# A two-layer streaming encoder: half-wide products in three PSUM banks, a second transpose bank, loads in place

## The chip, the cores and the metric

The kernel runs on one core of one Trainium2 chip. The metric is the device time of one execution in microseconds (us): the span from the program's first to its last instruction and what lies around it. Several executions are timed and their median is taken. A profile is one further execution with its own time.

## The reference

One inference step of a trunk of two layers, model width 2048, all in float32. 512 prompt frames and 64 sample frames go through together, 576 tokens. Layer 1 has stick-breaking attention (16 heads of 64) beside a Mamba-2 block (32 heads of 64, state 128); layer 2 has chunk-band attention (32 heads of 64, own chunk of 64 and 8 chunks back, a relative bias per head). Each layer has one input projection, SiLU gates, one output projection and a LayerNorm. Cut to what matters here:

```python
def odd_layer(x, past_k, past_v, w_in, rel_bias, w_out, ln_g, ln_b):
    q, k, v, g = jnp.split(jnp.einsum('bld,de->ble', x, w_in), 4, axis=-1)
    o = chunk_band_attention(q, k, v, past_k, past_v, rel_bias) * jax.nn.silu(g)
    y = layer_norm(DEEPNORM_ALPHA * x + jnp.einsum('ble,ed->bld', o, w_out), ln_g, ln_b)
# per head and block of 64 queries, inside chunk_band_attention:
    s = jnp.where(mc, einsum('bqhd,bkhd->bhqk', qc, kc) * CA_HEAD_DIM ** -0.5 + bias, -inf)
    out = einsum('bhqk,bkhd->bqhd', softmax(s), vc)
```

The outputs are the new activations, the new key and value rows, and the new states.

## The kernel before, in words

**Layout.** Activations stand transposed: 16 tiles of 128 features by 576 tokens. A **product** (`product`, `terms`, L107 to L124) makes 128 output features: two weight tiles of 128x1024 are loaded to `raw` (two buffers, 512 KB each, on SP's queue), and `split` (L88 to L94) makes a high part on ScalarE (`wh`, L93) and the rest on VectorE (`wl`, L94), three buffers each. For each of 16 blocks of 128 features three matmuls (high x high, high x low, low x high) run on each half of the tokens, 288 columns each: 96 matmuls. The two halves lie in two neighbouring banks of one `pj` tile. There are two `pj` tiles, four of the eight PSUM banks.

**Order.** The program is written in one order of pairs and steps, and a scheduler lays out each engine's list when the kernel is built, by a timing of its own. It fills waits of one step with instructions of others, such as matmuls of later products. On the chip every engine and queue follows its list strictly.

**Stages, in order of time in the span.**
- 0 to 655 us: layer 1's Mamba block. 655 to 1180: layer 1's attention, 8 pairs of heads.
- 1150 to 1500: `mix_norm` (L736 on): `bring` loads 24 stored tiles, 8 of them through two staging tiles `raws` and 16 through the unused tiles `d[4:]`, into high and low tiles `oh`, `ol` (L758 to L760). The output projection then runs. Its last `NHALF0 = 6` output tiles are made half by half of the tokens (L834): first half of all six, its statistics, then the second half, while VectorE and ScalarE normalise the first half. Weights of these tiles are loaded and split once for each half.
- 1490 to 1545: `two_of_seven` (L162): 2 block products for each of the first five query/key pairs, on the first token half alone, with results kept in `vs` tiles and stored. Then `early_values`: three value products.
- 1580 to 1925: `seven` (L176): query and key projections of layer 2 by a scheme with 7 block products (M1 to M7) of 24 matmuls for 16 pairs; the first five pairs have M1 and M2 already. A block product waits for a sum of weight tiles on VectorE and their split. For early pairs M7 and M4 go into the same bank `pa`, with the add at L223 reading it in between.
- 1925 to 2520: layer 2's attention, 16 pairs (`run_pairs`, L608). For each pair: `ca_heads` loads operands and makes the value product (evicted as `vf` at L534). Then the gate product, except for pairs in `GLATE`, whose gate comes after all pairs. `silu` reads the gate's `pj` tile three times (L130, L133, L135) and writes `gt`, of which there is one buffer. `ca_attend`: scores `z` (L490, two banks), softmax (L1057 to L1065), transposes of the weights (`transpose_tile`, `transpose_cached`, `transpose_new`, L571 to L589) into one bank with the tag `t`, from which VectorE (L567) and ScalarE (L569) evict by turns, then the product with the values (`po`, L596). `place` multiplies with `gt` (L636, L643).
- 2520 to the end: layer 2's `mix_norm`, with `NHALF1 = 3`, and the final norm: subtractions on GpSimd (L890), multiplications on VectorE (L891), scale and shift on ScalarE (L895), stores (L897).

**Queues.** Loads are issued by SP, all stores by GpSimd's queue (`store`, L58).

**PSUM in layer 2's attention:** four banks in two `pj` tiles, two for scores, one for `po` and the turned values, one for transposes.

Of the kernel before, what the change touches and what calls it, by code (L numbers as in the profile page):

```python
# [14 lines left out]
P = 128  # L15
# [13 lines left out]
GLATE = (10, 12, 14, 15)  # L29
NHALF0, NHALF1 = 6, 3  # L30
# [19 lines left out]
def encoder(ctx: ExitStack, tc: tile.TileContext, a):  # L50
# [7 lines left out]
    store = nc.gpsimd.dma_start  # L58
# [103 lines left out]
    def two_of_seven(w, m0, x1, x2, pl, dst):  # L162
# [5 lines left out]
        m1, c11 = (pl.tile([P, HALF], F32, tag="vs", name="vs", bufs=3) for _ in range(2))  # L168
# [7 lines left out]
    def seven(wa, m0, wb, m1, sums, ps, tmp, last=False, early=None):  # L176
# [21 lines left out]
        c11, c12, c21, c22 = o0[:, H0], o0[:, H1], o1[:, H0], o1[:, H1]  # L198
        if early is None:
            a12 = raw(wa, m0, 1, "raw", wpool, 2)  # L200
# [6 lines left out]
            pb = bank("pb")  # L207
            block(pb, a12, sums["M2"])
            tt(c11, c11, pb, ALU.add)
        else:  # L210
# [3 lines left out]
            a12 = raw(wa, m0, 1, "raw", wpool, 2)  # L214
# [9 lines left out]
        if last:  # L224
            tt(c21, c21, pa, ALU.add)
        tt(s_, a12, s_, ALU.subtract)
        block(pc, s_, sums["M3"], False, True)
        tt(c12, c12, pc, ALU.add)
        if not last:
            block(pa, a22, sums["M4"], False, True)  # L230
            out(c21, pa)
# [332 lines left out]
    def evict(dst, src):  # L564
        flip[0] ^= 1
        if flip[0]:
            nc.vector.tensor_copy(dst, src)  # L567
        else:
            act(dst, src, AF.Copy)  # L569

    def transpose_tile(wsrc, r, t, wts, flipq=False):  # L571

        nb = t + 1
        tp = pm.tile([P, 512], F32, tag="t", name="tpw")
# [5 lines left out]
    def transpose_new(wsrc, dst):  # L580
        tp = pm.tile([P, 512], F32, tag="t", name="tpn")
        nc.tensor.transpose(tp[0:TS, 0:P], wsrc, ident)
        evict(dst, tp[0:TS, 0:P])

    def transpose_cached(wsrc, dst):
        tp = pm.tile([P, 512], F32, tag="t", name="tpw")
# [21 lines left out]
    def run_pairs(lt, npair, late, heads, attend, wg, gate0, scr):  # L608
        pend = []
        for pr in range(npair):  # L610
            st = heads(pr)
            if pr not in late:
                pg = product(wg, gate0 + pr, 2, xh, xl)
                gt = lt.tile([P, T], F32, tag="gt", name="gt", bufs=1)
                silu(lt, pg, gt, T, "st")
# [7 lines left out]
        for pr, o in pend:  # L623
            pg = product(wg, gate0 + pr, 2, xh, xl)
            gt = lt.tile([P, T], F32, tag="gt", name="gt", bufs=1)
            silu(lt, pg, gt, T, "st")
            tt(o, o, gt, ALU.mult)
# [100 lines left out]
    run_pairs(bl_, NPAIR_SB, range(4, 8), sb_heads, sb_attend, a["w_in0"], 24, o_scr0[16:24])  # L728
# [7 lines left out]
    def mix_norm(nk, scr, w, res, gcol, bcol, cut, nhalf, out, beside=None):  # L736
# [9 lines left out]
        ddp = pool("dd", bufs=1, side="left")  # L746
        dd = ddp.tile([P, NK, T], F32, name="d")
        d = [dd[:, m, :] for m in range(NK)]
# [4 lines left out]
        def bring(pl, ks, stage):  # L753
# [8 lines left out]
        bring(oa, range(3), raws)  # L762
        ob = pool("ob", bufs=1, side="left")
        bring(ob, range(3, 8), raws)
        dp = pool("d", bufs=1, side="left")
        s1, s2, cm, mu = (dp.tile([P, T], F32, name=n) for n in ("s1", "s2", "cm", "mu"))
        bring(orr, range(8, nk), d[4:])
# [93 lines left out]
        def norm(ms, v):  # L861

            r = dd[:, ms.start:ms.stop, v]
# [8 lines left out]
        if inner:  # L872
            yp = pool("x1", bufs=1, side="right")
            yh, yl = (yp.tile([P, NK, T], F32R, name=n) for n in ("yh", "yl"))
            steps = beside(yh, yl, dp)
# [9 lines left out]
        else:  # L885
            for h, v in enumerate(toks):
                for m in range(NK):
# [8 lines left out]
                    if m % 2:  # L896
                        store(out[m - 1:m + 1, :, v].rearrange("m p t -> p m t"), dd[:, m - 1:m + 1, v])  # L897
# [5 lines left out]
        ob.release()  # L903
        oa.release()
        if inner:
            return yp, yh, yl, ddp, dd
        ddp.release()

    def early_pairs(hi, lo, pl):
        x = [[(hi[:, 8 * u + k, H0], lo[:, 8 * u + k, H0]) for k in range(8)] for u in range(2)]  # L910
        for pr in range(NAHEAD):
            yield from two_of_seven(a["w_in1"], pr, *x, pl, e_scr[pr])

    xp, yh, yl, ddp, ys = mix_norm(24, o_scr0, a["w_out0"], a["xT"], V_G0, V_B0, HALF, NHALF0, y_scr,
# [5 lines left out]
    vp = pool("vs", bufs=1, side="left")  # L920
# [286 lines left out]
```

## Time and profile before

| what | value |
|---|---|
| median of 3 runs (lowest, highest) | 2764.26 us (2759.38, 2769.35) |
| the profiled execution | 2769.17 us |
| its span | 2767.2 us |
| mean granted TensorE clock | 0.983 of full speed |
| TensorE busy (PE) | 2663.6 us, 96% |
| VectorE (DVE), ScalarE (ACT), GpSimd (POOL) busy | 59%, 43%, 8% |

Busy time of an engine is the time in which at least one of its instructions ran. Matmuls overlap each other in the trace, so their durations are longer than the distance from one to the next. "Idle before" a group of instructions names what ended the wait. The clock's two levels are 2.4 and 1.2 GHz; a clock of 0.94 for a stretch is a mean over parts at one level and at the other.

### The profile page before, as it was taken

How to read it: one execution, taken by the hardware profiler on the slowest of the kernel's cores; microseconds unless marked ns; L12 is line 12 of the kernel's file. 1: busy time of each engine (PE TensorE's matmuls, PEld its weight loads, DVE VectorE, ACT ScalarE, POOL GpSimd, SP SyncE). 2: the span in 40 equal slices, each digit the busy share in tenths (PEclk: the TensorE clock that was granted, in tenths of full speed). 3: DMA queues.
4: the chain of work that ended last, by engine and by line, in shares of the span. 5: the costliest groups of instructions: out<-in, count | busy, mean ns of one | idle time of the engine just before them, and what ended most of it. 6: DMA issues, size and time to landing. Idle time of an engine off the chain costs nothing.

```text
span 2767.2 us, 47827 instructions
## 1 busy us (share of the span) xinstructions
PE 2663.6 (96%) x19742; PEld 2536.1 (92%) x19742; DVE 1626.2 (59%) x2504; ACT 1197.1 (43%) x1976; POOL 209.3 (8%) x402
## 2 busy tenths in 40 slices
PE   8999999999999999999998899999999999998995
PEld 8999898999999999999998899999998899887995
DVE  6665656665556766643356677666555544564546
ACT  5434343434555665622244434444444433453224
POOL 0000010000000000000000111111000000000005
PEclk9999999999999999999999899999999999999998
DMA  5222232223323222443355565444745555544333
GB/s 186 77 88 80 65 102 65 94 70 118 97 90 97 97 90 90 155 128 101 101 175 171 171 200 175 159 158 161 227 141 155 162 151 162 154 129 154 107 108 120
DMA packets 126953, 355.07 MB, mean 128 GB/s; under 512 B 22400, under 2 KB 29184, under 8 KB 126736
## 3 DMA queue, kind: packets, MB, share of 16 engines
q1 hardware_dynamic: 107424, 286.40, 33.6%
q0 software_dynamic: 19312, 65.63, 6.1%
q8 instruction: 155, 2.54, 0.4%
q14 instruction: 62, 0.51, 0.1%
HBM read 286.34 MB, written 65.61 MB: 127 GB/s over the span
## 4 chain that ended last, share of the span: by engine, by line
PE 87%; DVE 5%; DMA 4%; ACT 2%; issue 1%; SPq 0%; POOLq 0%; POOL 0%; DVEq 0%; ACTq 0%
PE pj L124 59%; PE pa L159 5%; PE po L596 3%; PE pc L159 3%; PE pj L834 2%; PE tpw L576 2%; DMA sr<-w_in 1%; DVE wl L94 1%; PE z L490 1%; PE px L834 1%; PE pb L159 1%; PE z L491 1%; PE px L124 1%; PE pe L159 1%; ACT wh L93 1%
## 5 line engine op out<-in xcount | busy, mean ns | idle before, releaser
L93 ACT ACTIVATE wh<-raw 128x1024 fp32r<-128x1024 f32 x381 | 402.7, 1058 | 743.9 <-PE pj L124 521.7
L94 DVE TENSOR_TENSOR wl<-raw,wh 128x1024 fp32r<-128x1024 f32 x381 | 467.3, 1227 | 426.3 <-ACT wh L93 421.1
L124 PE MATMUL pj<-yh,wh 128*128 128x288 f32 x1024 | 227.0, 300 | 4.9 <-DVE vf L534 3.6
L124 PE MATMUL pj<-yh,wl 128*128 128x288 f32 x1024 | 225.0, 297 | 0.0
L124 PE MATMUL pj<-yl,wh 128*128 128x288 f32 x1024 | 223.3, 298 | 0.0
L124 PE MATMUL pj<-oh,wh 128*128 128x288 f32 x816 | 175.1, 297 | 5.9 <-ACT oh L759 4.0
L124 PE MATMUL pj<-ol,wh 128*128 128x288 f32 x816 | 175.4, 296 | 0.3 <-DVE ol L760 0.3
L124 PEld LDWEIGHTS pj<-yh,wh 128*128 128x128 f32 x1024 | 165.9, 188 | 9.6 <-DVE vf L534 5.0
L124 PE MATMUL pj<-oh,wl 128*128 128x288 f32 x816 | 174.5, 296 | 0.0
L124 PEld LDWEIGHTS pj<-yl,wh 128*128 128x128 f32 x1024 | 166.2, 188 | 2.1
L124 PEld LDWEIGHTS pj<-yh,wl 128*128 128x128 f32 x1024 | 166.9, 188 | 0.9
L124 PEld LDWEIGHTS pj<-oh,wh 128*128 128x128 f32 x816 | 131.4, 189 | 7.3 <-ACT oh L759 4.7
L124 PEld LDWEIGHTS pj<-ol,wh 128*128 128x128 f32 x816 | 131.5, 189 | 0.6 <-DVE ol L760 0.5
L124 PEld LDWEIGHTS pj<-oh,wl 128*128 128x128 f32 x816 | 131.9, 189 | 0.0
L567 DVE COPY wts<-tpw 128x128 f32<-128x128 f32 (+1 forms) x96 | 46.9, 488 | 113.0 <-PE tpw L576 112.8
L1061 ACT ACTIVATE t<-t,smx 128x128 f32<-128x128 f32 (+3 forms) x128 | 71.3, 558 | 50.9 <-DVE smx L1057 50.6
L596 PE MATMUL po<-wts,vt 128*64 128x512 f32 (+3 forms) x384 | 86.6, 460 | 0.0
L1057 DVE CUSTOM_DVE_ANT_0 t<-z,bp 128x128 f32<-128x128 f32 (+3 forms) x128 | 60.8, 486 | 43.0 <-PE tpw L576 33.0
L834 PE MATMUL pj<-oh,wh 128*128 128x288 f32 (+2 forms) x256 | 77.4, 302 | 5.1 <-DVE d L783 2.6
L834 PE MATMUL pj<-oh,wl 128*128 128x288 f32 (+2 forms) x256 | 77.4, 302 | 2.0 <-DVE wl L94 2.0
L834 PE MATMUL pj<-ol,wh 128*128 128x288 f32 (+2 forms) x256 | 76.2, 298 | 0.0
L490 PE MATMUL z<-kh,q 128*128 128x128 f32 (+1 forms) x192 | 66.5, 360 | 6.6 <-DVE smx L1057 5.1
(572 smaller groups left out, 7380.7 us busy)
## 6 DMA issues: line engine op xcount, KB each, us to landing
raw<-w_in SPq DMA_DIRECT2D x234, 512.0 KB, 3.6
raw<-w_out SPq DMA_DIRECT2D x104, 512.0 KB, 3.6
sr<-w_in SPq DMA_DIRECT2D x48, 512.0 KB, 4.3
q<-q_scr SPq DMA_DIRECT2D x64, 128.0 KB, 3.5
kh<-k_scr SPq DMA_DIRECT2D x64, 128.0 KB, 3.4
xr<-xT SPq DMA_DIRECT2D x26, 288.0 KB, 6.0
o_scr<-of POOLq DMA_DIRECT2D x24, 288.0 KB, 3.6
d<-o_scr SPq DMA_DIRECT2D x24, 288.0 KB, 5.6
```

The source lines that it names most:

```text
L93: act(hi, src, AF.Copy)
L94: tt(lo, src, hi.bitcast(F32), ALU.subtract)
L124: mm(ps[:, at.start + v.start:at.start + v.stop], st[:, c], mv[u * 8 + k][:, v], start=(first and k == 0 and i == 0), stop=(last and k == ...
L159: mm(acc, st[:, c], mv, start=(first and k == 0 and i == 0), stop=(k == 7 and i == 2), skip_group_check=more)
L490: mm(dst, q, kh, start=True, stop=False)
L491: mm(dst, q, kl, start=False, stop=True)
L567: nc.vector.tensor_copy(dst, src)
L576: nc.tensor.transpose(tp[:, b * P:(b + 1) * P], wsrc[:, b * P:(b + 1) * P], ident)
L596: mm(po[q, b * P:TP], vt[:, b, q], wts[:, b, r, b * P:TP], start=(b == 0), stop=(b == 3))
L834: mm(ps[i], st[:, c], mv, start=(u == order[0] and k == 0 and j == 0), stop=(u == 0 and k == 7 and j == 2))
L1057: nc.vector.tensor_tensor_reduce(t[:, i, at:at + z.shape[1]], z, b, -1.0, 3e38 if j == 0 else sm[:, i:i + 1], ALU.add, ALU.min, sm[:, i:i ...
L1061: act(t[:, i, :], t[:, i, :], AF.Exp, scale=-1.0, bias=sm[:, i:i + 1], accum_out=sm[:, 2 + i:3 + i])
```

## The change

1. Stores are issued by ScalarE's queue.
2. `seven` is reordered: for early pairs M3 comes ahead of M7, and M4 has a bank of its own, `pb`; for the others M2 follows M6. The tile `a12` is loaded first.
3. In `mix_norm` each stored tile is loaded straight into its `ol` tile and converted there; `d` is four tiles of four instead of one; `NHALF0` is 3. The tiles kept by `two_of_seven` and `early_values` come from two `stage` tiles, and the memory under them is laid out in another order (`oa` below `d`).
4. Layer 2's value and gate products run one token half after the other, in three banks by turns. The fourth bank of the two tiles is a second transpose bank, used by turns. Late gates are those of pairs 9, 11, 13, 15.

```diff
-GLATE = (10, 12, 14, 15)
-NHALF0, NHALF1 = 6, 3
+GLATE = (9, 11, 13, 15)
+NHALF0, NHALF1 = 3, 3
...
-    store = nc.gpsimd.dma_start
+    store = nc.scalar.dma_start
...
+        a12 = raw(wa, m0, 1, "raw", wpool, 2)
         if early is None:
...
-            pb = bank("pb")
-            block(pb, a12, sums["M2"])
-            tt(c11, c11, pb, ALU.add)
...
         block(pa, s_, sums["M6"], early is not None, early is None)
         out(c12, pa)
+        tt(s_, a12, s_, ALU.subtract)
+        pb = bank("pb")
+        if early is None:
+            block(pb, a12, sums["M2"])
+            tt(c11, c11, pb, ALU.add)
+        else:
+            block(pc, s_, sums["M3"], False, True)
+            tt(c12, c12, pc, ALU.add)
         tt(a21, a11, a21, ALU.subtract)
         block(pa, a21, sums["M7"], False, True)
         tt(c22, c22, pa, ALU.add)
...
+        else:
+            tt(c21, u1, pa, ALU.add)
+            block(pb, a22, sums["M4"])
+            tt(c21, c21, pb, ALU.add)
...
+    def tbank(name):
+
+        if spare:
+            flip[0] ^= 2
+            if flip[0] & 2:
+                return spare[0]
+        return pm.tile([P, 512], F32, tag="t", name=name)
...
-        raws = [oa.tile([P, T], F32, name=f"or{k}") for k in range(2)]
...
-                raw = stage[k % len(stage)]
+                raw = lo[k].bitcast(F32)
                 load(raw, scr[k])
                 act(hi[k], raw, AF.Copy)
                 tt(lo[k], raw, hi[k].bitcast(F32), ALU.subtract)
...
+        stage = [oa.tile([P, T], F32, name=f"stage{i}") for i in range(2)] if inner else None
+        bring(oa, range(1))
+        ddp = pool("dd", bufs=1, side="left")
+        dg = [ddp.tile([P, 4, T], F32, name=f"d{g}") for g in range(4)]
...
+    x0, x1 = (pj.tile([P, 1024], F32, tag="pj", name="pj") for _ in range(2))
+    hbanks, second = [x0[:, 0:HALF], x0[:, 512:512 + HALF], x1[:, 0:HALF]], x1[:, 512:1024]
+    turn_ = [0]
+
+    def product_halves(w, m):
+
+        ws = [wparts(w, m, u) for u in range(2)]
+        accs = []
+        for v in (H0, H1):
+            acc = hbanks[turn_[0] % 3]
+            turn_[0] += 1
+            for u, (wh, wl) in enumerate(ws):
+                for k in range(8):
+                    c = slice(k * P, (k + 1) * P)
+                    x, y = xh[8 * u + k][:, v], xl[8 * u + k][:, v]
+                    for i, (st, mv) in enumerate(((wh, x), (wh, y), (wl, x))):
+                        mm(acc, st[:, c], mv, start=(u == 0 and k == 0 and i == 0), stop=(u == 1 and k == 7 and i == 2))
+            accs.append((v, acc))
+        return accs
+
+    def silu_halves(pl, accs, dst, tag):
+        t = pl.tile([P, 580], F32, tag=tag, name=tag, bufs=2)[:, :T]
+        for v, p in accs:
+            act(t[:, v], p, AF.Abs)
+        act(t, t, AF.Exp, scale=-1.0)
+        act(t, t, AF.Ln, bias=one1)
+        for v, p in accs:
+            stt(t[:, v], p, 0.0, t[:, v], ALU.min, ALU.subtract)
+        act(t, t, AF.Exp)
+        for v, p in accs:
+            tt(dst[:, v], p, t[:, v], ALU.mult)
+
     pm = pool("pmc", bufs=1, space=PSUM)
+    spare.append(second)
```

## Rows read from the trace of the kernel before

**Rows 1.** The page: the span, and busy time of each engine.

```profile
span 2767.2 us, 47827 instructions
PE 2663.6 (96%) x19742; PEld 2536.1 (92%) x19742; DVE 1626.2 (59%) x2504; ACT 1197.1 (43%) x1976; POOL 209.3 (8%) x402
```

**Rows 2.** Stretches: length, PE, PEld, DVE, ACT, POOL busy, clock, DMA share, GB/s.

```profile
1366.00:1500.00 134.00, 125.40 (x901) 121.64 (x900) 80.07 (x95) 57.48 (x73) 3.58 (x5) 0.99 0.54 170
1500.00:1580.00 80.00, 73.14 (x512) 71.57 (x511) 53.96 (x47) 38.54 (x49) 10.09 (x17) 0.96 0.48 158
1580.00:1700.00 120.00, 108.73 (x780) 107.11 (x779) 87.83 (x99) 45.45 (x56) 22.07 (x41) 0.94 0.61 202
1700.00:1925.00 225.00, 223.61 (x1678) 222.28 (x1677) 152.64 (x164) 101.13 (x147) 35.47 (x66) 1.00 0.46 153
1925.00:2450.00 525.00, 509.62 (x3750) 464.87 (x3749) 271.39 (x723) 220.90 (x505) 35.57 (x68) 0.99 0.55 167
2450.00:2520.00 70.00, 61.42 (x427) 50.06 (x425) 39.87 (x107) 31.98 (x75) 3.23 (x6) 0.90 0.38 121
```

**Rows 3.** The chain that ended last: one whole product of 96 matmuls (start, us).

```profile
1192.78 12.93 PE pj L124 x96
```

**Rows 4.** TensorE's waits, 1160 to 1190 us: us in total, times, longest.

```profile
PE pj L124 <- ACT oh L759: 3.1, 1, 3.1
```

**Rows 5.** Three short stretches, columns as in rows 2.

```profile
1505.00:1545.00 40.00, 33.14 (x218) 31.99 (x217) 37.35 (x36) 24.57 (x37) 7.95 (x13) 0.91 0.60 195
1582.50:1592.70 10.20, 5.71 (x22) 5.37 (x23) 7.35 (x7) 3.06 (x3) 0.10 (x1) 0.50 0.68 209
2504.10:2517.70 13.60, 9.42 (x29) 5.02 (x31) 3.60 (x10) 2.45 (x6) 0.14 (x1) 0.50 0.53 179
```

**Rows 6.** TensorE's waits, 1366 to 1700 us: us in total, times, longest.

```profile
PE pc L159 <- ACT wh L93: 6.0, 1, 6.0
PE pa L159 <- DVE so L223: 4.8, 5, 2.2
PE pe L159 <- DVE vs L173: 3.3, 1, 3.3
```

**Rows 7.** SP's queue, its waits from 1570 to 1590 us.

```profile
SPq L182 <- DVE yl L951: 19.4, 1, 19.4
```

**Rows 8.** Timeline of VectorE (start, us): the last read of a gate's banks.

```profile
2042.04 0.76 DVE L135 TENSOR_TENSOR gt<-pj,st 128x576 f32<-128x576 f32 x1
```

**Rows 9.** Timeline of TensorE, 2502 to 2515 us: the last pair ([idle before]).

```profile
2509.86 1.11 PE L576 MATMUL tpw<-cst,t 128*128 128x128 f32 x4 [1.07 <-DVE wts L567]
2511.66 0.90 PE L576 MATMUL tpw<-cst,t 128*128 128x128 f32 x3 [0.69 <-ACT wts L569]
```

**Rows 10.** Timeline of TensorE, 2441 to 2452 us: two batches of transposes.

```profile
2444.60 0.38 PE L576 MATMUL tpw<-cst,t 128*128 128x128 f32 x2
...
2448.02 0.38 PE L576 MATMUL tpw<-cst,t 128*128 128x128 f32 x2
```

**Rows 11.** DMA issues: first and last of 23 lines of stores, 262 in all.

```profile
o_scr<-of POOLq DMA_DIRECT2D x24, 288.0 KB, 3.6
...
o_conv<-cvo POOLq DMA_DIRECT2D x1, 72.0 KB, 3.4
```

**Rows 12.** Timeline of SP's queue, 2038 to 2042 us: two issues.

```profile
2039.92 0.59 SPq L1015 DMA_DIRECT2D kl<-k_scr  x1
2041.50 0.33 SPq L1044 DMA_DIRECT2D cv<-cav  x1
```

**Rows 13.** Timeline of GpSimd, 2715 to 2768 us: the final norm.

```profile
2744.06 9.35 POOL L890 TENSOR_TENSOR d<-d,mu 128x256 f32<-128x256 f32 x11 [2.38 <-DVE mu L856]
2753.36 1.45 POOL L897 DMA_DIRECT2D o_y<-d  x2
2754.82 0.76 POOL L890 TENSOR_TENSOR d<-d,mu 128x256 f32<-128x256 f32 x1
```

**Rows 14.** Timeline of ScalarE: a gate's first read of its banks.

```profile
2005.92 0.63 ACT L130 ACTIVATE st<-pj 128x576 f32<-128x576 f32 x1
```

More of the change, by code (lines that the diff above doesn't have):

```diff
@@ L167, in two_of_seven @@
         yield
-        m1, c11 = (pl.tile([P, HALF], F32, tag="vs", name="vs", bufs=3) for _ in range(2))
+        m1, c11 = pl
         act(m1, pa, AF.Copy)
@@ L223, in seven @@
         tt(c22, c22, pa, ALU.add)
[L224 to L231, printed above, removed]
+        if early is None:
+            if last:
+                tt(c21, c21, pa, ALU.add)
+            block(pc, s_, sums["M3"], False, True)
+            tt(c12, c12, pc, ALU.add)
+            if not last:
+                block(pa, a22, sums["M4"], False, True)
+                act(c21, pa, AF.Copy)
+        else:
+            tt(c21, u1, pa, ALU.add)
+            block(pb, a22, sums["M4"])
+            tt(c21, c21, pb, ALU.add)
         return o0, o1
@@ L606, in sample_pv, with run_pairs @@
         return po[:, 0:TS]
-    def run_pairs(lt, npair, late, heads, attend, wg, gate0, scr):
+    def run_pairs(lt, npair, late, heads, attend, gate, scr):
         pend = []
@@ L612, in run_pairs @@
             if pr not in late:
-                pg = product(wg, gate0 + pr, 2, xh, xl)
-                gt = lt.tile([P, T], F32, tag="gt", name="gt", bufs=1)
-                silu(lt, pg, gt, T, "st")
+                gt = gate(lt, pr)
             else:
@@ L623, in run_pairs @@
         for pr, o in pend:
[L624 to L627, printed above, removed]
+            tt(o, o, gate(lt, pr), ALU.mult)
             store(scr[pr], o)
@@ L745, in mix_norm, with bring @@
         orr = pool("or", bufs=1, side="right")
-        ddp = pool("dd", bufs=1, side="left")
-        dd = ddp.tile([P, NK, T], F32, name="d")
-        d = [dd[:, m, :] for m in range(NK)]
         oa = pool("oa", bufs=1, side="left")
-        raws = [oa.tile([P, T], F32, name=f"or{k}") for k in range(2)]
         hi, lo = [None] * nk, [None] * nk
-        def bring(pl, ks, stage):
+        def bring(pl, ks):
             for k in ks:
@@ L861, in norm @@
         def norm(ms, v):
-            r = dd[:, ms.start:ms.stop, v]
+            r = dg[ms.start // 4][:, :, v]
             n = [[0, ms.stop - ms.start], [1, v.stop - v.start]]
@@ L874, in mix_norm @@
             yh, yl = (yp.tile([P, NK, T], F32R, name=n) for n in ("yh", "yl"))
-            steps = beside(yh, yl, dp)
+            steps = beside(yh, yl, stage)
             for h, v in enumerate(toks):
@@ L911, in early_pairs @@
         for pr in range(NAHEAD):
-            yield from two_of_seven(a["w_in1"], pr, *x, pl, e_scr[pr])
-    xp, yh, yl, ddp, ys = mix_norm(24, o_scr0, a["w_out0"], a["xT"], V_G0, V_B0, HALF, NHALF0, y_scr,
+            t = pl[pr % 2]
+            yield from two_of_seven(a["w_in1"], pr, *x, (t[:, H0], t[:, H1]), e_scr[pr])
+    xp, yh, yl, left, ys, stage = mix_norm(24, o_scr0, a["w_out0"], a["xT"], V_G0, V_B0, HALF, NHALF0, y_scr,
                                    early_pairs)
@@ L928, in early_values @@
                     yield
-            vs = vp.tile([P, T], F32, tag="vs", name="vs", bufs=2)
+            vs = stage[i % 2]
             act(vs, ps[:, parts(HALF)[1]], AF.Copy)
```

57 lines of the change are left out of this document (35 added, 22 removed).

## The prediction

> **What bounds the kernel now.** I read the page first: TensorE is busy for 2663.6 of 2767.2 us [rows 1], and the change takes no matmul away. What can be won is TensorE's 103.6 idle us and what it loses at the lower clock. The view by stretches says where: 8.6, 6.9 and 11.3 us idle between 1366 and 1700 us, 15.4 and 8.6 us in layer 2's attention, and 1.4 us in the 225 us between [rows 2]. There the clock falls too: 0.96 over 80 us costs 3.2 us of work, 0.94 over 120 us 7.2, 0.90 over 70 us 7.0, 0.99 over 525 us 5.3. A whole product lasts 12.9 us, a half 6.5 [rows 3]. Then the waits of each stretch, and the timeline around the longest.
>
> All terms are set against the profiled execution, 2769.2 us, whose span is 2767.2 us. It is 4.9 us over the median of the runs, 2764.3, so 4.9 us come off at the end. What a measurement can tell from no change is 0.3%, about 8.3 us.
>
> **The change part by part.**
>
> *Loads in place, layer 1.* Eight operand tiles no longer go through two staging tiles by turns, each reload waiting for a conversion. TensorE waited 3.1 us for such a tile [rows 4]. All loads can now go as soon as their own memory is free, which is when the attention ends; layer 1's late gate products cover them. The loads that used `d[4:]` ahead of time now start later, and could hold up weight loads behind them on SP's queue. Best: -3.1, and half as much again for the clock that fell beside it, so -5. Worst: one weight load late by its own wait, +5. I take -3. In layer 2 this costs nothing: the first operands cover the loads of the later ones.
>
> *NHALF0 from 6 to 3.* Three output tiles leave the half-by-half part. Each half step there has a weight tile for only 24 matmuls, 3.2 us. That is 9 loads and splits less. TensorE idles 8.6 us there [rows 2]; half of the steps stay, so -4. But the first half's norm then has 3 x 9.7 = 29 us of second-half matmuls beside it in place of 58. VectorE is already the bound just behind: busy for 37.35 of 40 us from 1505 to 1545 [rows 5]. Ends: -8 and +10.
>
> *Early pairs, `two_of_seven`.* Results lie in four half tiles in place of three, and ScalarE's copy waits for a store less often. TensorE waited 3.3 us for VectorE's add here [rows 6], and 6.9 us in all [rows 2]. The add was late because VectorE was full, and that stays. I take -2; ends -8 and +8.
>
> *Start of `seven`.* The first three weight tiles were issued when VectorE had read the last of `d` [rows 7], for they use its memory. TensorE then stood 6.0 us [rows 6], and the next 10.2 us ran at clock 0.50 [rows 5], of which the 5.7 busy us lost 2.9. With `d` in four tiles and the stage tiles below, the two weight tiles that M5 needs lie over memory that is free earlier; the third lies over the stage tile of the last early value and comes later, beside M5. So this wait goes, and with it the clock's fall: -9. What is late next is M6, by its own load. Best: -9; worst: the third tile holds it up as long as before, 0.
>
> *Order in `seven`.* M4 in its own bank needs no wait for the add at L223, 4.8 us in five waits [rows 6]. The longest was 2.2 us, but M3 ahead of M7 gives `out` cover too. I take -3; ends -5 and +1. One add more for each of five early pairs, at most 0.76 us each [rows 8], is covered: VectorE is idle for 32 of 120 us [rows 2]. The order of the other pairs gains nothing: TensorE is full there (223.6 of 225 us).
>
> *Second transpose bank, halves in three banks.* With one bank, a transpose waits until the last one is evicted. In the last pair, where no product is left to fill, this is a wait of 0.7 to 1.1 us at each of some nine transposes [rows 9], and TensorE falls to clock 0.50 for 13.6 us, with 9.42 us busy [rows 5]. Two banks evicted by two engines let the next transposes run beside the eviction. There I take -7: 4.2 us idle and part of 4.7 us of clock. In the pairs before, the lists put some 24 product matmuls, 3.4 us, between two such transposes [rows 10]. With about ten of them a pair's attention lasts as long as its two products and its own work. With two banks attention can run faster than that, and short waits inside it go. Of 15.4 idle us and 5.3 us of clock [rows 2] I take -11. Ends for both together: -37 (all idle and clock) and +10. More instructions in `silu_halves` and the two half evictions, at most 5 for each pair of 0.76 us [rows 8], lie beside products: VectorE and ScalarE are busy for 271 and 221 of 525 us.
>
> *Late gates 9, 11, 13, 15.* As many late gates as before, at other places. One fewer is left for the end, which the last item has in it: 0.
>
> *Stores on ScalarE.* 262 stores [rows 11] leave GpSimd. SP's issues last 0.33 to 0.59 us [rows 12], so ScalarE gets 86 to 155 us on top of 1197 [rows 1], 46 to 49% of the span. No issue by ScalarE is in this trace. Behind a store stand the next weight split's high part and the softmax exponentials; VectorE's low part and then TensorE wait for these. Three buffers of split weights cover 6 us or more. Ends: 0 and +39, a quarter of 155 us. I take +5, near the low end, because ScalarE is idle for more than half of every stretch. At the end of the kernel it is a gain: GpSimd's last subtraction stands 1.45 us behind two stores [rows 13], and its last stores end the span. I take -3; ends -5 and +2.
>
> A store's wait matters here more than its length. SP's trace shows an issue that stands 19.4 us for its memory [rows 7], with all later ones behind it. The Trainium skill, "DMA: Bandwidth & Descriptors", section on the anatomy of one DMA, says the same in general: a DMA engine waits for no semaphore; the wait is on the sequencer that issues, before dispatch. By that rule ScalarE would stop at every store whose data is late, where GpSimd had nothing else to do; the trace agrees for SP, and for ScalarE nothing here shows it. The stall of ScalarE is the third rival below.
>
> **The sum.** -3 - 4 - 2 - 9 - 3 - 7 - 11 + 5 - 3 = -37 us: 2732 us on the profiled execution, 2727 as a median.
>
> **The rivals.**
>
> *VectorE binds the shorter half part.* For it: 37.35 of 40 busy us [rows 5], and the norm's work stays while the matmuls beside it halve. Against it: the norm of the second half may spill into the early values, where there is room. NHALF0's and the early pairs' terms become +10 in place of -6: 2748, as a median 2743.
>
> *The second bank changes little.* The lists may still put 3.4 us of products between transposes [rows 10], since the scheduler's timing, not the chip's, sets them. Then only the last pair's 7 us remain: -26, 2743, as a median 2738.
>
> *Stores hold ScalarE.* +39 in place of +5: 2766, as a median 2761, no change.
>
> *Slower: gates starve the products.* A gate's banks are read for the first time at 2005.9 and last at 2042.0 us [rows 8, 14], because `gt` has one buffer that the pair before still needs. Meanwhile the other `pj` tile took two whole products. Now a gate holds two of three banks and only one half product, 6.5 us, can be made meanwhile. This decides as soon as fill runs out before the pair's attention ends. A pair then pays what the last one pays: 4.2 us idle and 4.7 us of clock. At half of the 12 early gates that is 53 us, and the 18 us of the transposes do not come: 2803, as a median 2798. Against it: faster attention frees `gt` sooner.
>
> *Slower: the clock.* If matmuls stop briefly at every change of banks, the clock of the last 70 us, 0.90 in place of 0.99 [rows 2], would hold for 595 us: +54 in place of -18, 2804, as a median 2799. The Trainium skill, "TensorE: Matmul & The Clock Gate", section on PSUM-queue depth-cycling, reports such a kernel: it cycles through banks, idles for very short times between groups, and its clock goes up and down. Here the trace differs: with banks changed after every product, the clock is 0.99 while products last.
>
> **How the numbers follow.** Chances: forecast 0.47; VectorE 0.18; second bank 0.13; stores 0.11; starving 0.08; clock 0.03. Two first rivals are faster as well, by 21 and 26 us, so faster is 0.79 with a little of the third; the third is the same; the last two, and a little of the third, are slower: 0.79, 0.10, 0.11. The range is 2693 to 2760. Below, the best ends of the attention (-37) and of the middle (-25), a little short of both; above, up to the third rival. Outside lie the two slow cases and about half of the third. Likeliest: 2727.
>
> **What would show it.** At the start of `seven` no wait for `wh` above 1 us, and clock 1.00 there. Waits for `so` L223 gone. From 1925 us: fewer product matmuls between transposes, idle under 1 us each in the last pair, clock above 0.95 in the last 70 us, and the stage some 18 us shorter. Output projection of layer 1 without the wait for `oh`. GpSimd without stores, and the last store issued earlier after the last subtraction. Wrong would be: VectorE full and TensorE waiting for `d` or `yh` from 1440 to 1540; TensorE idle in attention with no product ready; ScalarE standing before stores while TensorE waits for `wh`.

## The result, and the profile after the change

The changed kernel takes 2792.86 us (median of 4 runs, 2790.80 to 2801.43) against 2764.87 us before: a ratio of 1.0108, with a 95% interval from 1.0080 to 1.0136. It is 28 us slower where 37 us less were forecast, and lies outside the range. The profiled execution has a span of 2789.8 us; the page answers to [rows 1]:

```profile
span 2789.8 us, 47678 instructions
PE 2662.2 (95%) x19742; PEld 2538.9 (91%) x19742; DVE 1610.5 (58%) x2520; ACT 1190.2 (43%) x1993; POOL 63.4 (2%) x140
```

TensorE's busy time is the same within 1.4 us; its idle time has grown from 103.6 to 127.6 us. To see where, I cut both traces at the same five instructions on TensorE: the first matmul of layer 1's output projection, the first block product M5, the last block product, and the last column sum of the last norm (lengths in us, read from TensorE's timeline):

| stage | before | after | difference |
|---|---|---|---|
| state-space layer and layer 1's attention | 1166.7 | 1164.3 | -2.4 |
| output projection 1, early pairs, early values | 419.8 | 425.9 | +6.1 |
| block products (seven) | 337.9 | 334.0 | -3.9 |
| layer 2's attention, gates, output projection 2 | 818.1 | 846.2 | +28.1 |
| tail: the last norm and its stores | 24.7 | 19.4 | -5.3 |
| span | 2767.2 | 2789.8 | +22.6 |

The view by stretches of the changed kernel answers to [rows 2] (length, then busy us of PE, PEld, DVE, ACT and POOL, the clock, DMA share, GB/s):

```profile
1164.30:1363.60 199.30, 199.30 (x1495) 199.09 (x1494) 80.67 (x93) 53.25 (x64) 0.00 (x0) 1.00 0.39 128
1363.60:1500.00 136.40, 129.15 (x922) 126.43 (x921) 71.42 (x79) 51.50 (x68) 0.00 (x0) 0.97 0.43 135
1500.00:1577.20 77.20, 64.93 (x442) 63.10 (x440) 44.95 (x38) 33.41 (x41) 0.00 (x0) 0.93 0.40 137
1577.20:1590.20 13.00, 0.06 (x2) 0.03 (x1) 2.36 (x2) 1.71 (x2) 0.00 (x0) 0.58 0.75 270
1590.20:1700.00 109.80, 105.22 (x755) 102.55 (x756) 85.91 (x102) 41.74 (x52) 0.00 (x0) 0.97 0.60 190
1700.00:1924.30 224.30, 224.30 (x1696) 224.30 (x1695) 155.58 (x167) 101.80 (x150) 0.52 (x1) 1.00 0.48 156
...
1924.30:2487.60 563.30, 525.93 (x3842) 472.27 (x3840) 286.70 (x832) 236.83 (x582) 2.00 (x6) 0.97 0.52 158
2487.60:2548.00 60.40, 49.24 (x338) 48.54 (x336) 21.16 (x30) 19.55 (x29) 0.00 (x0) 0.89 0.30 97
```

Four things are to be seen. The output projection is now full (first row). From 1364 to 1577 us 19.5 us are idle. At 1577 us TensorE stands for 13 us. And layer 2's attention proper ends sooner, 563.3 us after its start in place of 594, but 60.4 us of gate products stand behind it where none did before; both stretches have idle time and a low clock. The attention proper of the kernel before, for comparison:

```profile
1924.40:2518.60 594.20, 570.96 (x4170) 515.05 (x4170) 310.76 (x829) 252.80 (x578) 38.80 (x74) 0.98 0.53 162
```

TensorE's waits there (us in total, times, longest) in the changed kernel:

```profile
PE pj L1028 <- DVE gt L1042: 16.3, 8, 6.0
PE z L498 <- DVE smx L1115: 9.3, 16, 1.5
PE tpw L594 <- ACT wss L577: 5.2, 7, 1.0
PE tpw L594 <- ACT wts L577: 4.9, 8, 1.5
```

At the head stands a product that waits for the gate's last read of its banks, 16.3 us. In the kernel before this wait was 1.1 us:

```profile
PE pj L124 <- DVE gt L135: 1.1, 4, 0.3
```

The timeline of the first of the gates left for the end shows how (start, length, engine, line; idle time and releaser in brackets): the product ends at 2494.3 us, the six steps of the gate (L1035 to L1042) follow on ScalarE and VectorE, and the next matmul begins when VectorE has read the first bank for the last time:

```profile
2493.97 0.29 PE L1028 MATMUL pj<-yh,wl 128*128 128x288 f32 x1
...
2495.14 0.39 ACT L1035 ACTIVATE st<-pj 128x288 f32<-128x288 f32 x1
...
2497.28 0.78 ACT L1037 ACTIVATE st<-st,cst 128x576 f32<-128x576 f32 x1
...
2498.08 0.82 DVE L1039 SCALAR_TENSOR_TENSOR st<-pj,st 128x288 f32<-128x288 f32 x2
...
2499.72 0.82 DVE L1042 TENSOR_TENSOR gt<-pj,st 128x288 f32<-128x288 f32 x2 [0.81 <-ACT st L1040]
...
2500.23 0.61 PE L1028 MATMUL pj<-yh,wh 128*128 128x288 f32 x1 [5.96 <-DVE gt L1042]
```

The last matmul took 0.29 us and the first one after the wait takes 0.61, and the granted clock from 2500 to 2510 us is 0.79: the wait costs clock as well.

### The profile page after: what moved, and what is told of

Read it like the earlier page. It is cut to its first block, busy times and chain, and to the rows that moved or that the text cites. A ratio compares the mean times of both kernels' runs of the same rounds, so it can differ in the third digit from the quotient of the medians.

```text
span 2789.8 us, 47678 instructions
## 1 busy us (share of the span) xinstructions
PE 2662.2 (95%) x19742; PEld 2538.9 (91%) x19742; DVE 1610.5 (58%) x2520; ACT 1190.2 (43%) x1993; POOL 63.4 (2%) x140
## 4 chain that ended last, share of the span: by engine, by line
PE 87%; DVE 5%; DMA 3%; ACT 3%; issue 2%; SPq 0%; ACTq 0%; DVEq 0%
PE pj L124 48%; PE pj L1028 13%; PE pa L159 5%; PE pc L159 3%; PE po L614 2%; PE pj L853 2%; PE pb L159 1%; PE tpw L594 1%; PE px L124 1%; ACT wh L93 1%; DVE wl L94 1%; PE z L498 1%; PE pos L623 1%; PE z L499 1%; DMA sr<-w_in 1%
## 5 line engine op out<-in xcount | busy, mean ns | idle before, releaser
L1028 PE MATMUL pj<-yh,wh 128*128 128x288 f32 x928 | 286.4, 309 | 18.9 <-DVE gt L1042 16.3
L1028 PE MATMUL pj<-yh,wl 128*128 128x288 f32 x928 | 283.7, 306 | 0.0
L1028 PE MATMUL pj<-yl,wh 128*128 128x288 f32 x928 | 282.9, 305 | 0.0
L124 PE MATMUL pj<-oh,wh 128*128 128x288 f32 x960 | 205.8, 296 | 0.0
L124 PE MATMUL pj<-ol,wh 128*128 128x288 f32 x960 | 205.8, 296 | 0.0
L124 PE MATMUL pj<-oh,wl 128*128 128x288 f32 x960 | 205.5, 295 | 0.0
L93 ACT ACTIVATE wh<-sr 128x1024 fp32r<-128x1024 f32 x43 | 45.1, 1057 | 63.9 <-PE pc L159 23.2
L614 PE MATMUL po<-wts,vt 128*64 128x384 f32 (+3 forms) x384 | 70.8, 441 | 1.1 <-DVE wts L575 1.1
L577 ACT ACTIVATE wts<-tpw 128x128 f32<-128x128 f32 (+1 forms) x96 | 41.3, 430 | 60.9 <-PE tpw L594 53.5
L499 PE MATMUL z<-kl,q 128*128 128x128 f32 (+1 forms) x192 | 61.1, 328 | 0.0
```

The source lines that it names most:

```text
L93: act(hi, src, AF.Copy)
L124: mm(ps[:, at.start + v.start:at.start + v.stop], st[:, c], mv[u * 8 + k][:, v], start=(first and k == 0 and i == 0), stop=(last and k == ...
L499: mm(dst, q, kl, start=False, stop=True)
L614: mm(po[q, b * P:TP], vt[:, b, q], wts[:, b, r, b * P:TP], start=(b == 0), stop=(b == 3))
L1028: mm(acc, st[:, c], mv, start=(u == 0 and k == 0 and i == 0), stop=(u == 1 and k == 7 and i == 2))
```

## The experiments

All ratios are against the kernel before, which had medians of 2761 to 2763 us beside these runs; kernels are compared with each other by their medians. Where a main stage is named, its length is that in the profiled execution, between the same cuts as in the table above.

**1. Release the gate's banks early.** The gate's product is copied to a second tile, and the rest of the gate works on the copy:

```diff
-        t = pl.tile([P, 580], F32, tag=tag, name=tag, bufs=2)[:, :T]
+        t, x = (pl.tile([P, 580], F32, tag=tag, name=tag, bufs=2)[:, :T] for _ in range(2))
         for v, p in accs:
             act(t[:, v], p, AF.Abs)
+            nc.vector.tensor_copy(x[:, v], p)
...
-        for v, p in accs:
-            stt(t[:, v], p, 0.0, t[:, v], ALU.min, ALU.subtract)
+        stt(t, x, 0.0, t, ALU.min, ALU.subtract)
...
```

> The changed kernel, but the gate of layer 2 is copied out of its two banks by VectorE while ScalarE takes the absolute value, so that the banks are free about 1 us after the product's end in place of some 5 us. Theory (gates hold two of three banks, and products starve): TensorE's 16.3 us of waits for the gate's last read go, with the lower clock behind them and most of the 59 us after the attention, so 15 to 30 us faster than the changed kernel: 2763 to 2778 us. Rival (the second bank and the new order of transposes cost the time, not the gates' banks): within 5 us of 2793.

Measured: 2725.20 us (ratio 0.9860, 0.9844 to 0.9877). That is 68 us less than the changed kernel, more than twice the upper end of what the theory allowed. TensorE's waits in its attention:

```profile
PE pj L1028 <- DVE st L1036: 4.2, 3, 2.4
PE pj L1028 <- ACT wh L93: 2.4, 2, 1.6
PE z L498 <- DVE smx L1114: 2.0, 6, 0.6
```

Attention, gates and output projection 2 as one stretch (columns as above), in this kernel:

```profile
1919.20:2703.00 783.80, 760.12 (x5732) 715.76 (x5732) 427.81 (x999) 326.12 (x696) 21.20 (x22) 0.99 0.51 157
```

and in the changed kernel:

```profile
1924.30:2770.00 845.70, 788.10 (x5733) 731.31 (x5732) 420.11 (x999) 324.05 (x697) 21.20 (x22) 0.97 0.47 146
```

Of the 61.9 us between the two rows, 33.9 are idle time of TensorE (57.6 against 23.7) and 28.0 are busy time for the same matmuls, at clock 0.97 in place of 0.99. With 16.3 us of direct waits thus went four times their length. The order of TensorE's instructions is not the same in the two kernels, so not all of it need come from the waits themselves. One way is likely but was not tested by itself: where no product could be started, the attention's own steps stand bare, and their short waits too.

**2. Undo the attention's part.** Whole products, one transpose bank, the old late gates; all else as changed:

```diff
-        accs = product_halves(a["w_in1"], 48 + pr)
+        pg = product(a["w_in1"], 48 + pr, 2, xh, xl)
...
-    spare.append(second)
```

> The changed kernel with the old attention of layer 2: whole products in two tiles, one transpose bank, late gates 10, 12, 14, 15. Theory (the whole loss lies in the attention of layer 2): 28 us off, 2765 us, equal to the kernel before. Rival (the middle part costs as well, and the attention of layer 2 was only given a worse start): 2775 or more.

Measured: 2760.35 us (0.9993, 0.9981 to 1.0006), equal to the kernel before. The loss lies in the attention of layer 2, and the rest of the change together is worth nothing that can be measured.

**3. Six half tiles again** (`NHALF0, NHALF1 = 6, 3`).

> The changed kernel with six half tiles in layer 1's output projection again, as before. Theory (three half tiles leave VectorE and the early pairs 58 - 29 us less cover, and TensorE waits from 1480 to 1540 us): 8 to 16 us faster, 2777 to 2785 us. Rival (the early pairs wait for the two shared stage tiles and for ScalarE, whatever the count of half tiles): within 4 us of 2793.

Measured: 2794.78 us (1.0115, 1.0097 to 1.0133). The rival holds: the count of half tiles changes nothing. TensorE's two largest waits between 1366 and 1580 us stay, here with six half tiles:

```profile
PE pe L159 <- ACT stage L169: 6.4, 3, 4.6
PE pe L159 <- DVE wl L94: 5.0, 2, 3.7
```

**4. The kernel before with its stores on ScalarE** (`store = nc.scalar.dma_start`).

> The kernel before with its 262 stores issued by ScalarE and nothing else changed. Theory (the first 650 us, in which only the stores differ, got 2 to 3 us shorter, and the end 5 us): 5 to 10 us faster, 2755 to 2760 us. Rival of the prediction (stores hold ScalarE): 2770 us or more.

Measured: 2760.69 us (0.9991, 0.9976 to 1.0007): no difference that is clear of one. ScalarE does stand before stores whose data is late; here it issues one only when VectorE has written `of`, at 815.6 us:

```profile
808.31 0.49 ACT L569 ACTIVATE wts<-tpw 128x384 f32<-128x384 f32 x1 [0.86 <-PE tpw L576]
815.66 0.33 ACTq L622 DMA_DIRECT2D o_scr<-of  x1
817.10 0.60 ACT L524 ACTIVATE vt<-tpv 128x512 f32<-128x512 f32 x1 [8.29 <-PE tpv L523]
```

Its next work waits for TensorE, and ScalarE is idle for the same 8.29 us at this place in the kernel before: the store stands in time that was idle anyway. The tail of this run is 19.2 us long, that of before 24.7, so the 5 us at the end are there. The 2 to 3 us in the first stage are not the stores': that stage takes 1163.3 us in run 8, where GpSimd issues them, and between 1162.7 and 1169.7 us over all the profiles.

**5 and 6. One transpose bank, four half banks**, with the gate copied out (5) and without (6):

```diff
-    hbanks, second = [x0[:, 0:HALF], x0[:, 512:512 + HALF], x1[:, 0:HALF]], x1[:, 512:1024]
+    hbanks, second = [x0[:, 0:HALF], x0[:, 512:512 + HALF], x1[:, 0:HALF], x1[:, 512:512 + HALF]], None
...
-            acc = hbanks[turn_[0] % 3]
+            acc = hbanks[turn_[0] % 4]
...
-    spare.append(second)
```

> The changed kernel with the gate copied out, and the second transpose bank given back: it becomes a fourth half bank for products. This leaves the halves and the early copy, and prices the second transpose bank. Theory (the second bank is worth the 18 us of the prediction once products are not starved): 2738 to 2748 us against 2725. Rival (the second bank is worth little, and the early release of the banks makes the whole gain): within 5 us of 2725.

> The changed kernel, the gate not copied out, with four half banks for products and one transpose bank. Theory (three banks are one too few while a gate holds two): TensorE's waits for the gate's last read go, 25 us or more off the changed kernel, 2768 us or less. Rival (the half products as such, or the longer gate with two instructions for each step, cost the time): within 8 us of 2793.

Measured: 2777.24 us (1.0055, 1.0039 to 1.0070) for 5 and 2758.98 us (0.9993, 0.9980 to 1.0006) for 6. With the early copy the second transpose bank is worth 52 us, not 18; without it, giving it back is worth 34 us. In TensorE's waits of run 6 the gate's falls from 16.3 to 1.4 us:

```profile
PE pj L1028 <- DVE gt L1042: 1.4, 5, 0.4
```

So neither halves nor the longer gate cost time by themselves. Why the early copy makes the kernel with four half banks 18 us slower is open.

**7. Other memory for the seven's first loads.** In the changed kernel the first weight load of the seven stands on SP's queue for the store of the last early value, because its tile lies over that value's. The waits of TensorE and of SP's queue there, in the changed kernel:

```profile
PE pc L159 <- ACT wh L93: 12.9, 1, 12.9
...
SPq L182 <- DMA o_cav<-stage: 14.5, 2, 13.9
```

and the timeline of ScalarE and SP:

```profile
1577.27 0.65 ACT L949 ACTIVATE stage<-pj 128x576 f32<-128x576 f32 x1 [5.23 <-PE pj L124]
...
1578.31 0.45 ACTq L951 DMA_DIRECT2D o_cav<-stage  x1
...
1580.80 1.28 SPq L182 DMA_DIRECT2D sr<-w_in  x3
```

The value is copied out of its bank at 1577.3 us, its second store lands at 1580.7, and only then three loads go. Two tiles that the seven needs late were put first, so that they lie over the stage tiles (on top of run 1):

```diff
     tm7 = pool("tm7", bufs=1, side="left")
+    for n in ("qh", "ql"):
+        tm7.tile([P, TP], F32R, tag=n, name=n, bufs=1)
```

> The changed kernel with the gate copied out, and two tiles that the seven products need late laid over the two stage tiles, so that their first weight loads use memory that is free earlier. Theory (the 12.9 us wait at the start of the seven is the first load standing behind the store of the last early value): that wait falls to 3 to 7 us and the time by 5 to 10 us, 2715 to 2720. Rival (another of the first loads, or VectorE's sum after them, is as late): within 3 us of 2725.

Measured: 2712.21 us (0.9819, 0.9803 to 0.9836), 13 us less than run 1. Theory, and somewhat more than it gave: the loads go at 1566.1 us, 0.2 us after the second store of the value before has landed (1565.9 us), so a store, an earlier one, may still be what releases them. Of the 12.9 us 2.7 are left, here in TensorE's waits of run 7:

```profile
PE pc L159 <- ACT wh L93: 2.7, 1, 2.7
```

**8. The kernel before with the early copy** (the edit of run 1, in the gate of whole products).

> The kernel before, with nothing changed but that the gates of layer 2 are copied out of their banks by VectorE while ScalarE takes the absolute value. Theory (holding a bank through the gate matters only where three half banks are left): within 6 us of 2763. Rival (the gate's hold was a limit before the change too, and halves and the second bank are not needed for the gain): 2745 us or less.

Measured: 2758.58 us (0.9980, 0.9969 to 0.9992). Theory: the gate's hold was no limit before the change.

**9. Two tiles for the gate's result** (`tag="gt", bufs=2` in layer 2, on the changed kernel).

> The changed kernel with two tiles for the gate's result in layer 2 in place of one. Theory (the gate's own chain of seven steps, 4 to 5 us from the end of its product to its last read of the banks, holds them): nothing changes, within 5 us of 2793. Rival, which is the reason given in the prediction (the gate waits for its one result tile, which the pair before still needs): the waits for the gate's last read go, 20 us or more off, 2773 us or less.

Measured: 2794.50 us (1.0112, 1.0085 to 1.0138), and in TensorE's waits of its attention the gate's is as long as it was:

```profile
PE pj L1028 <- DVE gt L1042: 17.3, 8, 6.5
```

The reason that the prediction gave for the starving, the single `gt`, falls.

**10 to 12. Three parts put back into run 7**: stores on GpSimd (10), the old order of block products (11), late gates 10, 12, 14, 15 (12). The edit of 11:

```diff
-        tt(s_, a12, s_, ALU.subtract)
-        pb = bank("pb")
         if early is None:
+            pb = bank("pb")
             block(pb, a12, sums["M2"])
...
-            tt(c21, u1, pa, ALU.add)
-            block(pb, a22, sums["M4"])
-            tt(c21, c21, pb, ALU.add)
+        if not last:
+            block(pa, a22, sums["M4"], False, True)
+            out(c21, pa)
```

> The best kernel so far (the change, the gate copied out, the seven's first loads over memory that is free early; 2712 us) with all stores issued by GpSimd again. Theory (ScalarE's stores gain 2 to 3 us in the first 650 us and 5 us at the end of the kernel, and cost nothing measurable between): 5 to 9 us slower, 2717 to 2721 us. Rival (they cost in the attention what they gain at the end): within 3 us of 2712.

> The same best kernel with the block products of the seven in their old order (M7 ahead of M3, the sum M4 last and in the bank of M7). Theory (the new order takes 3 to 5 us of waits for an add away): 2715 to 2718 us. Rival (those waits are filled by other blocks anyhow): within 2 us of 2712.

> The same best kernel with the late gates 10, 12, 14, 15 of before in place of 9, 11, 13, 15. Theory (as many late gates, so as much fill): within 5 us of 2712. Rival (which pairs lend their gates decides where fill runs out): 8 us or more slower, 2720 us or more.

Measured: 2719.26 us (0.9842, 0.9820 to 0.9863), 2717.11 us (0.9842, 0.9808 to 0.9876; its runs lie 19 us apart) and 2721.57 us (0.9850, 0.9827 to 0.9872). Stores: 7 us, with 4.8 us of it in the tail (24.5 against 19.7 us in the two profiles), as the theory has it. Order of the blocks: not settled by the times; the stage of block products is 335.1 us long against 333.6. Late gates: 9 us slower, which is what the rival asked for, though only 6.7 of them lie in the attention (785.2 against 778.5) and the first stage, where the edit does nothing, is 5.3 us longer in this profile.

**13. The edit of run 7 alone**, on the changed kernel.

> The changed kernel with nothing but two later tiles laid over the two stage tiles (the gate still holds its banks). Theory (the wait at the start of the seven, 12.9 us, is a loss of its own beside the attention's): 8 to 13 us off the changed kernel, 2780 to 2785 us, the same step as with the gate copied out. Rival (what the seven gains is lost again in the starved attention): within 4 us of 2793.

Measured: 2783.75 us (1.0080, 1.0060 to 1.0100), 9 us less than the changed kernel, and its slowest run (2789.83 us) is faster than the fastest of that kernel (2790.80): a loss of its own. Not all of the gain arrives, though: in the profiled execution (2787.3 us) the stage before the block products is 11.0 us shorter than in the changed kernel and the attention 7.2 us longer.

**14 and 15. Early pairs**, on run 7: three half tiles of their own (14), the projection's output in one tile again (15):

```diff
...
-            t = pl[pr % 2]
-            yield from two_of_seven(a["w_in1"], pr, *x, (t[:, H0], t[:, H1]), e_scr[pr])
+            t = [pl.tile([P, HALF], F32, tag="vs", name="vs", bufs=3) for _ in range(2)]
+            yield from two_of_seven(a["w_in1"], pr, *x, t, e_scr[pr])
```

```diff
-        dg = [ddp.tile([P, 4, T], F32, name=f"d{g}") for g in range(4)]
+        dd = ddp.tile([P, NK, T], F32, name="d")
+        dg = [dd[:, 4 * g:4 * g + 4, :] for g in range(4)]
```

> The best kernel so far (2712 us) with three half tiles of their own for the early pairs, as before, in place of the two shared stage tiles. Theory A (the early pairs of the change wait for the two shared tiles and the stores that read them): 3 to 6 us faster, TensorE's waits from 1440 to 1560 us fall from 17.5 to some 10 us. Theory B (VectorE's and ScalarE's sums and splits, which come earlier with four tiles of d, stand ahead of the weight splits): within 2 us of 2712 and the same waits.

> The best kernel so far (2712 us) with the output of the projection in one tile in place of four. Theory B (with four tiles the sums for the seven start 13 us earlier, at 1506 in place of 1519 us, and push the weight splits back while VectorE is full): 3 to 6 us faster there, and TensorE's waits from 1440 to 1560 us fall from 17.5 to some 10 us; the start of the seven may give some of it back. Theory A (the two shared stage tiles): within 2 us of 2712 or slower, the same waits from 1440 to 1560 us.

Measured: 2708.49 us (0.9809, 0.9793 to 0.9825) and 2717.03 us (0.9836, 0.9820 to 0.9852). Between 1440 and 1560 us the changed kernel's waits for `pe` are these, and below them those of run 14:

```profile
PE pe L159 <- DVE wl L94: 6.2, 2, 4.3
PE pe L159 <- ACT stage L169: 4.6, 3, 2.3
PE pe L159 <- ACT wh L93: 2.8, 1, 2.8
```

```profile
PE pe L159 <- ACT wh L93: 2.8, 1, 2.8
PE pe L159 <- ACT vs L169: 2.6, 3, 1.6
PE pe L159 <- DVE wl L94: 1.9, 1, 1.9
```

Own tiles take 6.0 us off that stage (413.4 to 407.4 us against run 7), and the waits for `pe` come to some 7 us, about what they were before the change: the shared stage tiles are the loss there. Run 15 does not test the other theory: the sums began at 1508 us with one tile too.

**16 to 18. A tile for each bank.** The waits in the changed program itself gave the reason that was still missing. This is its list around 2200 us, each row a run of product matmuls (start of the first and of the last) or a read (its start), with its times in the trace, the tile and the place in it (0 or 512, one bank each), and the instruction waited for:

```
2188.2-2196.5  PE x48      x0 at 512   second half of a value product
2198.8-2214.5  PE x96      x1 at 0, x0 at 0   a gate
2219.78        DVE L1042   x1 at 0     its reads, the last
2220.16        DVE L1042   x0 at 0
2220.7-2230.6  PE x48      x0 at 512   next gate; waits for L1042, x0 at 0
2238.1-2244.9  PE x48      x1 at 0     its second half
2250.46        DVE L1042   x0 at 512   its reads
2250.83        DVE L1042   x1 at 0
2251.0-2259.4  PE x48      x0 at 0     a value; waits for L1042, x0 at 512
```

The last row writes a bank that was read for the last time at 2220.6 us, 30 us earlier, and waits for a read of the other bank of its tile. The three half banks are parts of two tiles, and the wait is kept by tile. Taken by turns, 12 of the 16 gates have one half in each tile, and such a gate stops every product until its end. With four half banks (run 6) the two halves of a product fill one tile, and no gate lies across. So the banks became four tiles: on the changed kernel (16), on run 14 (17), and with four banks for halves and one for transposes (18):

```diff
-    x0, x1 = (pj.tile([P, 1024], F32, tag="pj", name="pj") for _ in range(2))
-    hbanks, second = [x0[:, 0:HALF], x0[:, 512:512 + HALF], x1[:, 0:HALF]], x1[:, 512:1024]
+    pj.release()
+    ph = pool("ph", bufs=1, space=PSUM)
+    b4 = [ph.tile([P, 512], F32, name=f"pj{i}") for i in range(4)]
+    hbanks, second = [t[:, 0:HALF] for t in b4[:3]], b4[3]
...
```

> The changed kernel, but the four banks of layer 2's products and transposes are four tiles of their own in place of halves of two tiles; the gate still holds its banks. Theory (waits are kept by tile: a gate whose halves lie in different tiles blocks all four banks, so a product also waits for a read of the other bank of its tile): most of the 16.3 us of waits for the gate's last read go and the time falls by 25 us or more, to 2768 us or less. Rival (three banks are too few while a gate holds two, whatever the tiles): within 8 us of 2793.

> The best kernel so far (2708 us: gate copied out, seven's first loads over memory free early, early pairs with tiles of their own) with the four banks as four tiles. Theory (early copy and own tiles take the same wait away, so one of them is enough): within 6 us of 2708. Rival (the transposes in the second bank still wait for products of its tile, and more is gained): 2700 us or less.

> The changed kernel with four tiles of a bank each, all four for half products, and one transpose bank, the gate not copied out; beside it the run with four half banks in two tiles had 2759 us. Theory (with four banks a product's halves fill a whole tile, so tiles of their own change little; and the second transpose bank is worth the 18 us of the prediction or more): within 6 us of 2759, and 18 us or more slower than the run with three bank tiles and a second transpose bank. Rival (tiles of their own are what counts and the second transpose bank is worth little): within 8 us of that run.

Measured: 2714.53 us (0.9831, 0.9813 to 0.9850), 2691.18 us (0.9745, 0.9729 to 0.9761) and 2757.11 us (0.9989, 0.9979 to 0.9999). Run 16 takes 78 us off the changed kernel without another edit, with three banks and the gate on its banks as long as before: the theory holds and three banks are enough. TensorE's waits in its attention:

```profile
PE pj L1030 <- ACT wh L93: 2.0, 2, 1.2
PE pj L1030 <- DVE gt L1044: 1.6, 1, 1.6
```

and that attention as one stretch:

```profile
1922.00:2440.00 518.00, 514.58 (x3988) 482.38 (x3987) 289.01 (x842) 240.70 (x591) 2.00 (x6) 1.00 0.57 175
```

16.3 us of waits for the gate are 1.6, and TensorE is busy for 514.58 of 518 us at full clock. Run 17 shows that early copy and own tiles are the same gain in the main but not wholly: where the copy is already there the tiles take off 17 us (against run 14), without it 78. It is the fastest kernel here, 70 us under the kernel before. Its page, and below it the attention and what follows as one stretch:

```profile
span 2688.6 us, 47651 instructions
PE 2622.8 (98%) x19742; PEld 2521.3 (94%) x19742; DVE 1617.5 (60%) x2520; ACT 1188.3 (44%) x1993; POOL 63.4 (2%) x140
```

```profile
1906.00:2500.00 594.00, 590.86 (x4564) 558.78 (x4564) 338.81 (x895) 272.69 (x633) 1.48 (x5) 1.00 0.57 175
```

Run 18 against 16 prices the second transpose bank with the tiles apart: 43 us.

## Why the prediction was wrong

**Second transpose bank, halves in three banks (-7 and -11).** This step failed: measured +28.1 us. It took for granted that each half bank comes free when its own reads are done; even the rival of starving let one half product run beside a gate. They come free by tile, and halves taken by turns put most gates across both tiles. The layout could have been seen, for the diff cuts three halves and a spare out of two tiles; that the waits go by tile no row of the kernel before shows. The mechanism of the term itself, shorter waits and a better clock with a second transpose bank, was right and too small: with the banks as tiles the stage is 768.0 us long in place of 818.1, 50 us less where 18 were forecast, and 817.3 with the second transpose bank given back (runs 16, 18). TensorE's idle time in it is 14.3 us (run 16) against 32.5 before, its busy time 753.7 against 784.5.

**The rival "gates starve the products"** came out, at 0.08. Its place and direction were right and its time, 2798 us, is 5 us off, but that nearness is luck, for its two reasons were not right: the single `gt` plays no part (run 9), and two of three banks held by a gate are no limit (run 16). It is a wait by tile, and each of the two edits that end it (runs 1 and 16) gives 68 us and more.

**Start of the seven (-9).** This step failed too: the wait went from 6.0 us [rows 6] to 12.9. I took the load that lies over the stage tile to come third, beside M5. The first of the three loads on SP's queue waits for the stage tile's store, and the other two stand behind it, as in [rows 7]. The rule of the Trainium skill that the prediction cited, in "DMA: Bandwidth & Descriptors", section on the anatomy of one DMA, that a wait stands on the issuing sequencer, agrees with these 13.9 us on SP, and with ScalarE's stand before its store in run 4. With the tiles moved 2.7 us are left (run 7), so against before 3.3 us and their clock could be won here; the forecast of all of it was too high as well.

**Half tiles (-4) and early pairs (-2).** The waits for `pe` from 1440 to 1560 us grew from some 8 us to 14, and the stage by 6.1 us with the start of the seven in it. Three or six half tiles make no difference (run 3), so both the term and the rival "VectorE binds the shorter half part" had the wrong cause; the cause is the two stage tiles shared with the early values, for with tiles of their own the waits are some 7 us again (run 14).

**Loads in place (-3):** right; 4.8 us of idle time in that stretch are none. **Order in the seven (-3):** the stage is 3.9 us shorter, but it is between 335.0 and 337.9 us in the four profiles with the old order (before, runs 4, 8 and 11) and between 333.0 and 335.4 in all others, so the order is worth some 2 us. The waits for the add, 4.8 us [rows 6], went as forecast; in their place stand waits for `wl`, which were 0.5 us. TensorE's waits for blocks from 1565 to 1700 us, after those 12.9 us:

```profile
PE pc L159 <- DVE wl L94: 3.2, 8, 0.6
PE pa L159 <- DVE wl L94: 1.3, 3, 0.5
```

**Stores on ScalarE (+5, and -3 at the end).** The tail is 5.3 us shorter, just over the best end of -5. The charge of 5 us was not seen: ScalarE does stand before late stores, at the place shown in time that was idle anyway (run 4), and its 262 issues cost nothing that shows. At the end GpSimd subtracts without a break, and ScalarE's last issue comes right behind its last result, in place of [rows 13]:

```profile
2771.74 10.22 POOL L909 TENSOR_TENSOR d<-d,mu 128x256 f32<-128x256 f32 x12 [7.87 <-DVE mu L875]
...
2785.95 0.90 ACTq L916 DMA_DIRECT2D o_y<-d  x2
```

**Late gates (0):** not nothing once the starving is gone; some 7 us in the attention hang on which pairs lend theirs (run 12).

**The clock.** The rival that a change of banks lowers it falls. In run 16 the banks change after every half for 518 us and the clock is 1.00, with 3.4 us idle; in the changed kernel the same turn of banks runs at 0.97, with 37.4 us idle in 563.3. The section on PSUM-queue depth-cycling of the Trainium skill's "TensorE: Matmul & The Clock Gate" lays a swinging clock to idle times between groups in a kernel that cycles through banks; these two runs agree as to the idle times, and show that the cycling alone does not bring them.

## What to carry to other kernels

Before parts of one tile are handed out by turns, look whether the program waits for the part or for the tile: here the same three banks made the kernel 28 us slower as parts of two tiles and 47 us faster as tiles of their own. A buffer that a long chain reads can be copied out at once where producers wait for it; that took off 68 us here, did next to nothing in the kernel before, and cost 18 us beside four half banks, so it has to be tried. The first loads of a stage should lie over memory that is free early: a store that still read that memory cost 9 to 13 us. A wait that holds TensorE can cost more than its length: with 16 us of them went 62, in other idle time and in busy time, where the order of instructions changed as well.

## What the runs showed of the hardware that was not expected

A TensorE that stands still again and again, up to 6 us at a time, pays for it in the matmuls behind: with the same matmuls (5733 and 5732 records) from the attention's start to the last norm, its busy time was 788.1 us in the changed kernel, at clock 0.97, and 760.1 in run 1, at 0.99. As an estimate from these two rows, 3% of 788.1 less 1% of 760.1, some 16 of the 28 us are clock; what the others are is open. And 262 DMA issues moved to ScalarE, 0.33 to 0.45 us each in the rows above, left the kernel's time where it was (run 4).
